# A decoder layer on one core: the feed-forward part as two stages of its own, its first product by Strassen's scheme

## The chip, the cores and the metric

The kernel runs on one core of one Trainium2 chip. The metric is the device time of one execution in microseconds. The time before is the median of three runs.

## What is computed

One inference step of a hybrid decoder layer, for a prompt of 2048 tokens and for 8 sample tokens, which share all weights. Everything is fp32. Cut to what matters here:

```python
h = rmsnorm(x)
u_ssm | u_pool | q_mem | gate_logits = h @ w_in
o_ssm  = S5 state-space model over time, GELU, GLU        # sequential over tokens
o_pool = trailing means of 2, 4, 8, 16 tokens, a linear map per group
o_mem  = cross-attention (4 heads) into 256 memory tokens; samples have their own cached keys and values
merged = sum_b sigmoid(gate_b) * (o_b @ w_branch_up[b])   # three branches
x = x + rmsnorm(merged @ w_out)
hf = rmsnorm(x) @ w_ffn_in                                # 1024 -> 2 x 2816
x = x + rmsnorm((silu(hf[:, :2816]) * hf[:, 2816:]) @ w_ffn_out)
```

## The kernel before, in words

Activations stand with the channel on the 128 partitions and tokens along the row. The prompt is worked in four blocks of 512 tokens (q = 0 to 3); the 8 sample tokens ride with block 1, which is therefore 520 wide and is computed in two column pieces of 256 and 264. fp32 accuracy comes from splitting each operand into a high and a low fp32r part (`split`, L167 to L169: ScalarE makes the high part, VectorE or, for the kinds in ON_POOL, GpSimd the low one), and three matmuls for each pair of tiles: high x high, high x low, low x high (`mmk`, L263). So a tile of 128 outputs over 1024 inputs is 8 x 3 matmuls for each column piece.

Weights come as tiles of at most 512 KB in one fixed order (`_weight_plan`), each loaded by SP and split three tiles ahead of its use (`wget`, `prefetch`, `w_emit`, L226 to L255), through four buffers each of wr, wh, wl. All DMAs are issued by SP.

Each block runs, in order: GLU of the S5 output; projections with memory attention and pooling (`projections`); gates and branch products for the three branches (`gates`, in block 0 in the order 2, 1, 0, later 0, 1, 2); the out-projection (`out_project`, L1187); the projection of u for the next block (`ssm_project`); then the residual with its norm (`residual`, L1204), which makes the split operand h2 of the feed-forward part. The feed-forward part follows for the same block in chunks of 5, 5, 6 and 6 column blocks: `ffn_in` (L1228) computes for each of 22 column blocks the gate half (fa) and the linear half (fb), 8 x 3 matmuls each, scales by the reciprocal norm, applies SiLU and splits the product; `ffn_out` (L1274) multiplies a chunk back, 8 output tiles, and adds the chunks in SBUF. `finish` (L1298) adds the last residual and stores.

Work that is not on the matmul stream is written as generators in a list called background; `step` issues the next piece of the first generator at marked places, `flush` all of what is left. The S5 recurrence of block q+1 (`s5_group`) is issued in steps within the feed-forward part of block q. `norm_stats` and `norm_apply` prepare the next block's input. In block 1 `sample_attention` (L1053) streams the samples' cached keys and values (56 transfers of 256 KB) in steps during the gates of branches 0 and 1; branch 2, which needs it, comes last. In the last block the out-projection and the last chunk of the second product run in two halves of 256 tokens, so that the tail is short.

The Tile framework orders each engine's instructions by a simulated time line with the order of writing as priority, and puts in the semaphores; PSUM has six banks under the tag pa and two under pb.

Of the kernel before, what the change touches and what calls it, by code (L numbers as in the profile page):

```python
# [19 lines left out]
P = 128  # L20
# [12 lines left out]
FCH = (5, 5, 6, 6)  # L33
FOFF = (0, 5, 10, 16)
# [9 lines left out]
STEPS = (1, 3, 1, 1)  # L44
# [4 lines left out]
NARROW = (QS, NQ - 1)  # L49
ORDER = ((2, 1, 0), (0, 1, 2), (0, 1, 2), (0, 1, 2))  # L50


def _weight_plan():
# [14 lines left out]
    ffn = []  # L68
    for c in range(len(FCH)):
        for f in range(FOFF[c], FOFF[c] + FCH[c]):  # L70
            ffn += [("fa", f), ("fb", f)]
        if c > 0:
            ffn += [("fo", c - 1, m) for m in range(KD)]
    ffn += [("fo", len(FCH) - 1, m) for m in range(KD)]
    seq = [("wk", h) for h in range(NH)] + [("wv", i) for i in range(4)] + us
    for q in range(NQ):
        if q > 0:
            seq += glu
        seq += proj
        for b in ORDER[q]:  # L80
            if q == 0 and b == 0:
                seq += glu
            seq += gates(b, q == 0 and b == 0)
        last = q + 1 == NQ
        seq += wo + wo if last else wo + us
        seq += ffn
        if last:
            seq += ffn[-KD:]
# [4 lines left out]
_STORED = [k for k in dict.fromkeys(_SEQ) if k[0] not in ("KT", "V")]  # L93
# [37 lines left out]
def trunk(ctx, tc, nc, I, O):  # L131
    V, S, G, T = nc.vector, nc.scalar, nc.gpsimd, Tensor(tc, nc)
    pool = ctx.enter_context(tc.tile_pool(name="sb", bufs=1))
# [3 lines left out]
    BUFS = {"h": 16, "br": 24, "acc": 8, "xr": 3, "U": 5, "G": 2, "tmp": 7, "rb": 1, "rb2": 1, "st2": 1,  # L137
            "ops": 6, "wr": 4, "wh": 4, "wl": 4}
    SIZE = {"tmp": 528, "ops": 512, "G": 512, "wr": 1024, "wh": 1024, "wl": 1024}
# [5 lines left out]
    def slot(tag, dt=F32):  # L145
        n = nm(tag)
        return pool.tile([P, SIZE.get(tag, W520)], dt, tag=tag, name=n, bufs=BUFS[tag])

    def small(shape, tag, bufs=1, dt=F32):
        n = nm(tag)  # L150
        return pool.tile(shape, dt, tag=tag, name=n, bufs=bufs)
# [31 lines left out]
    g_pre, g_post, g_fpre, g_fpost, g_mem = (gv[:, i, :] for i in range(5))  # L183
    cv = small([P, 2, NB], "cv")
# [14 lines left out]
    d_rb = dram([NQ, P, W520], "d_rb")  # L199

# [22 lines left out]
    seq = _SEQ  # L223
    wstate = {"emit": 0, "cur": 0, "buf": {}}

    def w_emit(i):  # L226
        key = seq[i]
        n = _ncols(key)
# [14 lines left out]
    def prefetch():  # L243
        i = wstate["cur"]
        while wstate["emit"] <= min(i + AHEAD, len(seq) - 1):
            w_emit(wstate["emit"])
            wstate["emit"] += 1
# [53 lines left out]
    def rsqrt_scaled(dst, sums, r, bl):  # L301
        v = slot("tmp")
        sl = slice(bl[0][0], bl[-1][0] + bl[-1][1])
        d, rr, vv = dst[:, sl], r[:, sl], v[:, sl]
        for o, n in bl:
            ps = psum2()
            T.matmul(ps[:, :n], lhsT=ones, rhs=sums[:, o:o + n], start=True, stop=True)
            V.tensor_tensor(v[:, o:o + n], r[:, o:o + n], ps[:, :n], MUL)
        V.tensor_tensor(vv, vv, rr, MUL)
        V.tensor_scalar(vv, vv, 1.0 / DM, EPS, MUL, ADD)  # L310
        rsqrt_core(d, vv, sl.stop - sl.start)
        V.tensor_tensor(d, d, rr, MUL)

    def rsqrt_rows(sums, bl, r=None):
        lo, hi = bl[0][0], bl[-1][0] + bl[-1][1]
        ns = -(-(hi - lo) // P)
# [4 lines left out]
        c = small([P, 3, 5], "rsq", 4)  # L321
        d, v, a = (c[:w, i, :ns] for i in range(3))
        if r is None:
            V.tensor_scalar(v, ps[:w, :ns], 1.0 / DM, EPS, MUL, ADD)
        else:
            V.tensor_tensor(v, ps[:w, :ns], r, MUL)
            V.tensor_tensor(v, v, r, MUL)
            V.tensor_scalar(v, v, 1.0 / DM, EPS, MUL, ADD)
# [6 lines left out]
        if r is not None:  # L335
            V.tensor_tensor(d, d, r, MUL)
# [715 lines left out]

    def sample_attention(qs, o_mem):  # L1053
# [7 lines left out]
        for b in range(NS):  # L1061
            qb = slot("U")
            nc.sync.dma_start(qb[:, :512].rearrange("p (h d) -> p h d", h=NH),
                              qv[b].unsqueeze(0).to_broadcast([P, NH, P]))
            for mt in range(2):
                kc = slot("U")
# [18 lines left out]
        for b in range(NS):  # L1085
            for hp in range(2):
                pb = slot("U")
                nc.sync.dma_start(pb[:, :512].rearrange("p (h m) -> p h m", h=2),
                                  dv[b, 2 * hp:2 * hp + 2].unsqueeze(0).to_broadcast([P, 2, NMEM]))
                vc = slot("U")  # L1090
# [4 lines left out]
        for m in range(NH):  # L1095
            hi, lo = o_mem[m]
            split(hi[:, TQ:W520], lo[:, TQ:W520], os_[:, :, m])
        yield

    def projections(q, h, br):  # L1100
# [3 lines left out]
        ns = 1 if q == 0 else 0  # L1104
# [39 lines left out]
    def gates(q, b, first, last, h, ob, acc, out, extra=None):  # L1144
        n = width(q)
        wub = None
        ahead = q == 0 and b == 0
# [39 lines left out]
    def out_project(q, mg, z, st, bl):  # L1187
        for m in range(KD):
            w = wget("wo", m)
            ps = [psum() for _ in bl]  # L1190
            mmk(q, ps, w, mg, bl=bl)
            if len(z) <= m:
                z.append(slot("acc"))
            sq = st if m == 0 else slot("tmp")
            for p_, (o, n) in zip(ps, bl):
                sl = slice(o, o + n)
                S.activation(sq[:, sl], p_[:, :n], AF.Square)  # L1197
                S.activation(z[m][:, sl], p_[:, :n], AF.Copy, scale=g_post[:, m:m + 1])
            sl = slice(bl[0][0], bl[-1][0] + bl[-1][1])
# [4 lines left out]
    def residual(q, z, st, st2, h2, bl):  # L1204
        rb = slot("rb")
        with T:
            (rsqrt_mean if q + 1 < NQ else rsqrt_quick)(rb, st, bl)
        yield
        sl = slice(bl[0][0], bl[-1][0] + bl[-1][1])
        for k in range(KD):  # L1210
# [318 lines left out]
```

## Time and profile before

| | |
|---|---|
| median of 3 runs | 3197.15 us (3193.63 to 3197.33) |
| span of the profiled execution | 3196.5 us; no separate time is listed for it, the median lies 0.65 us above |
| mean granted TensorE clock | 0.983 |
| moved by DMA | 393 MB, 123 GB/s mean |

The rows further down are read so: engines are PE (TensorE matmuls), PEld (its weight loads, which overlap), DVE (VectorE), ACT (ScalarE), POOL (GpSimd) and SP (which issues DMAs). L119 is the one line at which every matmul is recorded, so matmuls are told apart by tile names and shapes. Idle time of an engine that does not set the end costs nothing.

### The profile page before, as it was taken

Reading aid. Unit: us, or ns where it says so; the run is one execution under the profiler, and the core shown is the slowest. Engines: PE = TensorE matmul, PEld = TensorE weight load, DVE = VectorE, ACT = ScalarE, POOL = GpSimd, SP = SyncE. Lnnn points to the kernel's source line nnn. Section 1 sums busy time; section 2 is a strip of 40 time slices with the busy share of each in tenths; the row PEclk is TensorE's granted clock in tenths of the full one; section 3 lists DMA queues with packets and bytes.
Section 4 is the critical chain, followed back from the end, with each engine's and each line's share of the span. In section 5 each row is a group of like instructions: output and inputs, shape, how many; then the busy total and the mean of one; then the engine's idle time right before and its main releaser. Section 6 shows DMA issues by size and latency. Waiting matters only on the chain.

```text
span 3196.5 us, 43801 instructions
## 1 busy us (share of the span) xinstructions
PE 3071.6 (96%) x17043; PEld 2651.8 (83%) x17043; DVE 1879.6 (59%) x2905; ACT 1122.9 (35%) x1791; POOL 855.7 (27%) x690
## 2 busy tenths in 40 slices
PE   8889999999989899899999999999999999999997
PEld 6778877888888799899998888788888788888887
DVE  7877768555485635755548544764556833563346
ACT  4532433322344224323224423433223522533222
POOL 2565242111154403211114311421112501620112
PEclk9999999999999999999999999999999999999999
DMA  6354444323347633433324432533323333432233
GB/s 204 110 167 136 143 127 141 112 88 106 100 144 178 212 98 119 142 95 113 109 76 142 153 112 92 165 114 114 106 86 125 125 99 95 146 124 92 90 115 105
DMA packets 174735, 393.14 MB, mean 123 GB/s; under 512 B 39680, under 2 KB 51520, under 8 KB 174528
## 3 DMA queue, kind: packets, MB, share of 16 engines
q1 hardware_dynamic: 174528, 390.35, 38.7%
q8 instruction: 134, 2.20, 0.3%
q14 instruction: 73, 0.60, 0.1%
HBM read 362.41 MB, written 27.55 MB: 122 GB/s over the span
## 4 chain that ended last, share of the span: by engine, by line
PE 83%; DVE 9%; DMA 3%; issue 1%; ACT 1%; POOL 1%; SPq 1%; DVEq 0%; POOLq 0%; ACTq 0%
PE pa L119 79%; PE pb L119 3%; DVE acc L1319 1%; PE pb L122 1%; DVE acc L1213 1%; DVE wl L169 1%; DVE tmp L419 1%; DMA U<-in_cv_t 1%; SPq L660 1%; DMA U<-in_ck 0%; DMA d_ops<-br 0%; DVE tmp L289 0%; DVE rb L290 0%; DMA ops<-d_ops 0%; DVE tmp L288 0%
## 5 line engine op out<-in xcount | busy, mean ns | idle before, releaser
L119 PE MATMUL pa<-h,wh 128*128 128x512 f32 (+2 forms) x6144 | 1568.3, 352 | 30.0 <-DVE h L1221 17.1
L119 PEld LDWEIGHTS pa<-h,wh 128*128 128x128 f32 x6144 | 1040.3, 191 | 189.9 <-DVE h L1221 19.6
L168 ACT ACTIVATE wh<-wr 128x1024 fp32r<-128x1024 f32 (+3 forms) x572 | 568.2, 994 | 1557.7 <-PE pa L119 1186.3
L119 PE MATMUL pa<-h,wl 128*128 128x512 f32 (+2 forms) x3072 | 983.5, 351 | 0.7 <-POOL wl L169 0.7
L119 PE MATMUL pa<-br,wh 128*128 128x512 f32 (+2 forms) x3848 | 929.8, 340 | 20.7 <-ACT wh L168 8.3
L169 DVE TENSOR_TENSOR wl<-wr,wh 128x1024 fp32r<-128x1024 f32 (+3 forms) x476 | 572.7, 1203 | 370.9 <-ACT wh L168 360.0
L119 PEld LDWEIGHTS pa<-br,wh 128*128 128x128 f32 x3848 | 635.5, 189 | 106.1 <-ACT wh L168 8.5
L119 PEld LDWEIGHTS pa<-h,wl 128*128 128x128 f32 x3072 | 546.5, 190 | 79.5 <-POOL wl L169 1.0
L119 PE MATMUL pa<-br,wl 128*128 128x512 f32 (+2 forms) x1924 | 596.2, 340 | 1.0 <-DVE wl L169 1.0
L1265 POOL TENSOR_TENSOR tmp<-tmp,tmp 128x512 f32<-128x512 f32 (+1 forms) x88 | 150.5, 1712 | 934.5 <-ACT tmp L1264 934.5
L169 POOL TENSOR_TENSOR wl<-wr,wh 128x1024 fp32r<-128x1024 f32 (+1 forms) x96 | 238.7, 2493 | 514.3 <-ACT wh L168 482.9
L119 PEld LDWEIGHTS pa<-br,wl 128*128 128x128 f32 x1924 | 340.7, 189 | 42.9 <-DVE wl L169 1.4
L1267 DVE TENSOR_TENSOR tmp<-tmp,pa 128x512 f32<-128x512 f32 (+1 forms) x110 | 61.8, 579 | 230.4 <-PE pa L119 225.8
L1263 DVE TENSOR_TENSOR tmp<-rb,pa 128x512 f32<-128x512 f32 (+1 forms) x110 | 61.5, 578 | 193.1 <-PE pa L119 188.2
L1288 DVE TENSOR_TENSOR acc<-acc,pa 128x512 f32<-128x512 f32 (+2 forms) x128 | 68.7, 552 | 152.5 <-PE pa L119 152.3
L1181 POOL TENSOR_TENSOR acc<-acc,tmp 128x512 f32<-128x512 f32 (+1 forms) x32 | 48.5, 1519 | 224.6 <-DVE tmp L1179 206.0
L168 ACT ACTIVATE br<-tmp 128x512 fp32r<-128x512 f32 (+1 forms) x120 | 75.7, 633 | 75.3 <-DVE tmp L1267 31.6
L169 DVE TENSOR_TENSOR br<-tmp,br 128x512 fp32r<-128x512 f32 (+1 forms) x120 | 90.6, 756 | 4.7 <-ACT br L168 4.5
L1201 DVE TENSOR_TENSOR tmp<-tmp,tmp 128x512 f32<-128x512 f32 (+2 forms) x35 | 62.9, 1796 | 48.7 <-ACT tmp L1197 48.6
L119 PE MATMUL pa<-wh,h 128*128 128x512 f32 x256 | 84.6, 406 | 4.4 <-DVE h L376 2.3
L1179 DVE TENSOR_TENSOR tmp<-tmp,pa 128x512 f32<-128x512 f32 (+1 forms) x80 | 44.8, 579 | 65.0 <-PE pa L119 63.6
L1214 POOL TENSOR_TENSOR acc<-acc,xr 128x512 f32<-128x512 f32 (+2 forms) x40 | 57.3, 1448 | 80.5 <-DVE acc L1213 61.0
(316 smaller groups left out, 2626.9 us busy)
## 6 DMA issues: line engine op xcount, KB each, us to landing
wr<-in_w_all SPq DMA_DIRECT2D x424, 512.0 KB, 3.4
ops<-d_ops SPq DMA_DIRECT2D x112, 256.0 KB, 3.6
wr<-in_w_all SPq DMA_DIRECT2D x72, 384.0 KB, 3.0
xr<-in_x_t SPq DMA_DIRECT2D x96, 256.0 KB, 3.5
wr<-in_w_all SPq DMA_DIRECT2D x64, 320.0 KB, 2.8
d_ops<-br SPq DMA_DIRECT2D x28, 256.0 KB, 2.7
out_y_t<-acc SPq DMA_DIRECT2D x24, 256.0 KB, 3.6
d_x<-acc SPq DMA_DIRECT2D x16, 256.0 KB, 3.3
```

The costliest lines, as they stand in the source:

```text
L119: self._done(self.nc.tensor.matmul(*a, **k))
L122: self._done(self.nc.tensor.transpose(*a, **k))
L168: S.activation(dst_hi, src, AF.Copy)
L169: (eng or V).tensor_tensor(dst_lo, src, f(dst_hi), SUB)
L1179: V.tensor_tensor(t[:, sl], t[:, sl], u_, MUL)
L1181: (V if last else G).tensor_tensor(acc[j][:, :n], acc[j][:, :n], t[:, :n], ADD)
L1201: V.tensor_tensor(st[:, sl], st[:, sl], sq[:, sl], ADD)
L1214: G.tensor_tensor(zk, zk, xt[:, sl], ADD)
L1263: V.tensor_tensor(t[:, sl], rb2[:, sl], a_, MUL)
L1265: G.tensor_tensor(t[:, :n], t[:, :n], sg[:, :n], MUL)
L1267: V.tensor_tensor(t[:, sl], t[:, sl], b_, MUL)
L1288: V.tensor_tensor(zz, zz, p_[:, :n], ADD)
```

## The change

The kernel becomes three stages. Stage one is the mixing part of all four blocks, one after another, each followed at once by the projection of u for the next. All blocks now take the branches in the order 2, 1, 0, with GLU ahead of branch 0; S5 and the residual of the block before are background work of the projections and gates, in more steps (STEPS, NS1). The samples' attention has to be complete ahead of the gates of branch 2, the first ones of block 1, and uses the eight acc buffers instead of the five U buffers. The residual now also writes the reciprocal norm to DRAM.

Stage two computes the first feed-forward product for two pairs of blocks, (0, 1) and (2, 3), 1024 tokens each; the samples are divided over blocks 0 and 1 (516 columns), blocks 2 and 3 have 512. `sums` (a background generator, for the first pair in stage one) scales the stored residuals, makes Strassen-Winograd's sums of token half and channel half, and stores seven operands of four tiles each in d_S. `left` loads and splits these 28 tiles through xr. For each of the 22 column blocks `w_pair` loads fa and fb and makes the sums of weights. Seven products of 4 k x 3 passes x 2 column halves are accumulated in three pairs of PSUM banks, of which X is read three times in between. The gated products go to DRAM (d_f).

Stage three runs the second product block by block over all 22 input tiles at once (`load_f`, 44 split tiles held), in two column halves side by side, for the last block one half after the other. SBUF of the stages is shared by pools that follow each other; a tile waits only for the tiles whose place it takes.

```diff
-FCH = (5, 5, 6, 6)
+FCH = (8, 8, 6)
+SB = ((0, 1), (2, 3))
-STEPS = (1, 3, 1, 1)
+STEPS = (1, 2, 2, 2)
+NS1 = (1, 7, 1, 1)
-ORDER = ((2, 1, 0), (0, 1, 2), (0, 1, 2), (0, 1, 2))
+ORDER = (2, 1, 0)
...
+    BUFS = {"U": 5, "G": 2, "ops": 6, "h": 16, "br": 24, "acc": 8, "rb2": 1,
+            "xr": 4, "tmp": 7, "rb": 1, "wr": 4, "wh": 4, "wl": 4, "wt": 2,
+            "ev": 4, "S": 56, "f": 52, "z": 8}
...
+    def w_pair(f):
+        wa, wb = w_load(("fa", f)), w_load(("fb", f))
+        t21, t34 = slot("wt"), slot("wt")
+        L, R = slice(0, BW), slice(BW, 2 * BW)
+        V.tensor_tensor(t21[:, R], wb[:, L], wa[:, L], SUB)
+        V.tensor_tensor(t21[:, L], wb[:, R], t21[:, R], SUB)
+        V.tensor_tensor(t34[:, L], wb[:, R], wb[:, L], SUB)
+        V.tensor_tensor(t34[:, R], wa[:, R], t21[:, L], SUB)
+        for src in (wa, t21, t34, wb[:, R]):
+            hi, lo = slot("wh", F32R), slot("wl", F32R)
+            split(hi[:, :n], lo[:, :n], src)
...
             if i == 3 and q == QS:
-                background.append(sample_attention(qs, o_mem))
-                step(2)
+                background.insert(len(background) - 1, sample_attention(qs, o_mem))
...
+    def sums(sb):                       # 4 k: four scaled tiles, four sums, seven stores
+            V.tensor_tensor(s1, A[1, 0], A[1, 1], ADD)
+            V.tensor_tensor(s3, A[0, 0], A[1, 0], SUB)
+            V.tensor_tensor(s2, s1, A[0, 0], SUB)
+            V.tensor_tensor(s4, A[0, 1], s2, SUB)
+            for i, t in enumerate((A[0, 0], A[0, 1], s4, A[1, 1], s1, s2, s3)):
+                nc.sync.dma_start(d_S[sb, i, k, :, :n], t)
...
+    PRODUCTS = (0, 1, 5, 4, 6, 3, 2)
+    def left(sb):
+        for i in PRODUCTS:
+            for k in range(KH):
+                raw = slot("xr")
+                nc.sync.dma_start(raw[:, :n], d_S[sb, i, k, :, :n])
+                hi, lo = slot("S", F32R), slot("S", F32R)
+                split(hi[:, :n], lo[:, :n], raw[:, :n])
...
+    def ffn_in(sb, got):                # for each of 22 column blocks f_
+            B11, B21, T2, T1, T3, t4, B22 = wget("f1", f_)
+            product(X, 0, B11, True)
+            take(p1)                    # ScalarE reads both banks of X
+            product(Z, 1, B21, True)
+            plus(p1, Z)                 # VectorE adds both banks of Z
+            step()
+            product(X, 5, T2, False)
+            take(u2)
+            product(Y, 4, T1, True)
+            step()
+            product(X, 6, T3, False)
+            take(u3)
+            plus(u3, Y)
+            product(X, 3, t4, False)
+            both(f1_)                   # sigmoid of X, times X
+            product(Y, 2, B22, False)
+            plus(u2, Y)
+            S.activation(f0[:, :n], p1[:, :n], AF.Sigmoid)
+            G.tensor_tensor(f0[:, :n], f0[:, :n], p1[:, :n], MUL)
+            for i, (ft, b) in enumerate(((f0, u2), (f1, u3))):
+                V.tensor_tensor(ft[:, :n], ft[:, :n], b[:, :n], MUL)
+                nc.sync.dma_start(d_f[SB[sb][i], f_, :, :n], ft[:, :n])
+            step()
...
     for q in range(NQ):
-        if q > 0:
-            br[0] = glu(q, yT)
-            step(1)
...
+            if b == 0:
                 flush()
                 br[0] = glu(q, yT)
             if b == 2 and q == QS:
-                flush()
+                while "samples" not in done:
+                    step()
...
+            if i == 0 and q + 1 == NQ:
+                background.append(sums(0))
...
+        out_project(q, mg, z, st)
+        flush()
+        res = residual(q, z, st)
         if q + 1 < NQ:
+            background.append(res)
             U, us = ssm_project(q + 1, h)
             background.append(s5(q + 1, U, us, yT))
+        else:
+            run(res)
...
+    for sb in range(len(SB)):
+        prefetch()
+        got = left(sb)
+        if sb + 1 < len(SB):
+            background.append(sums(sb + 1))
+        ffn_in(sb, got)
+        flush()
...
+    for q in range(NQ):
+        ft = load_f(q, n)
+        for bl in ([[(0, n // 2), (n // 2, n // 2)]] if q + 1 < NQ else [[x] for x in HALVES]):
+            ffn_out(ft, bl, z, st)
+            flush()
+            background.append(finish(q, z, st, bl))
```

## Rows read from the trace of the kernel before

**Rows 1.** The page, busy time of each engine with share of the span.

```profile
PE 3071.6 (96%) x17043; PEld 2651.8 (83%) x17043; DVE 1879.6 (59%) x2905; ACT 1122.9 (35%) x1791; POOL 855.7 (27%) x690
```

**Rows 2.** The chain of waits: start us, us, what; block 0, block 1, the last half.

```profile
801.35 89.13 PE pa L119 x384
...
1330.19 46.09 PE pa L119 x384
...
3142.91 21.03 PE pa L119 x177
```

**Rows 3.** The page's costliest groups: busy us, mean ns | idle before; weight loads.

```profile
L119 PEld LDWEIGHTS pa<-h,wh 128*128 128x128 f32 x6144 | 1040.3, 191 | 189.9 <-DVE h L1221 19.6
```

**Rows 4.** Stretches at hand-overs: length, busy PE, PEld, DVE, ACT, POOL, clock, DMA, GB/s.

```profile
889.00:952.00 63.00, 53.69 (x396) 51.97 (x395) 56.90 (x79) 29.84 (x67) 30.27 (x19) 0.92 0.48 151
...
1268.00:1315.00 47.00, 40.60 (x240) 36.21 (x238) 39.73 (x49) 18.78 (x38) 14.32 (x9) 0.93 0.50 154
...
1705.00:1760.00 55.00, 48.32 (x217) 39.86 (x217) 52.30 (x64) 24.19 (x47) 26.68 (x15) 0.91 0.45 143
...
2040.00:2090.00 50.00, 43.32 (x180) 34.09 (x179) 41.86 (x47) 19.74 (x41) 16.23 (x9) 0.93 0.46 154
...
2458.00:2513.00 55.00, 47.83 (x206) 38.90 (x205) 52.64 (x61) 23.46 (x44) 29.11 (x16) 0.91 0.46 147
...
2799.00:2842.00 43.00, 37.99 (x252) 35.02 (x253) 29.23 (x71) 14.28 (x28) 6.41 (x8) 0.92 0.46 147
```

**Rows 5.** The same view: block 0's S5, block 1's samples, block 2's gates, its feed-forward.

```profile
112.00:250.00 138.00, 118.93 (x559) 96.83 (x558) 106.90 (x291) 51.19 (x89) 87.40 (x185) 0.94 0.47 147
...
952.00:1004.00 52.00, 45.51 (x345) 44.12 (x345) 34.53 (x61) 28.59 (x60) 30.00 (x28) 0.97 0.67 155
1004.00:1115.00 111.00, 95.68 (x753) 94.19 (x752) 61.24 (x87) 26.01 (x46) 49.28 (x35) 0.94 0.69 207
...
1800.00:1996.00 196.00, 196.00 (x845) 158.27 (x844) 81.75 (x87) 59.48 (x75) 26.61 (x17) 1.00 0.33 105
...
2090.00:2458.00 368.00, 368.00 (x1685) 301.37 (x1684) 202.94 (x280) 114.80 (x154) 62.31 (x37) 1.00 0.34 108
```

**Rows 6.** Groups by line and shape, VectorE: busy us, mean ns | idle before.

```profile
L169 DVE TENSOR_TENSOR wl<-wr,wh 128x1024 fp32r<-128x1024 f32 x344 | 454.3, 1321 | 334.0 <-ACT wh L168 323.7 <-PE pa L119 5.7
L169 DVE TENSOR_TENSOR br<-tmp,br 128x512 fp32r<-128x512 f32 x90 | 68.4, 762 | 2.5 <-ACT br L168 2.5
...
L795 DVE TENSOR_TENSOR_SCAN G<-r,carry_re,G 128x128 f32<-128x128 f32 x64 | 44.2, 746 | 7.9 <-POOL G L788 7.8
...
L289 DVE TENSOR_TENSOR tmp<-tmp,tmp 128x512 f32<-128x512 f32 x24 | 21.8, 907 | 0.5
...
L1213 DVE TENSOR_TENSOR acc<-acc,rb 128x512 f32<-128x512 f32 x16 | 20.8, 1368 | 0.1
...
L1288 DVE TENSOR_TENSOR acc<-acc,pa 128x256 f32<-128x256 f32 x40 | 16.7, 417 | 41.4 <-PE pa L119 41.2
...
L784 DVE TENSOR_TENSOR G<-ops,pb 128x512 f32<-128x512 f32 x16 | 11.0, 686 | 7.1 <-PE pb L119 3.9 <-DMA ops<-d_ops 2.9
```

**Rows 7.** The same view, ScalarE.

```profile
L168 ACT ACTIVATE wh<-wr 128x1024 fp32r<-128x1024 f32 x432 | 457.4, 1060 | 1164.9 <-PE pa L119 846.8 <-issue 275.3 <-POOL acc L1320 14.2
...
L168 ACT ACTIVATE br<-tmp 128x512 fp32r<-128x512 f32 x90 | 56.6, 631 | 53.4 <-DVE tmp L1267 24.0 <-DVE tmp L960 21.0 <-DVE tmp L917 7.5
...
L1178 ACT ACTIVATE tmp<-pa 128x256 f32<-128x256 f32 x16 | 5.8, 365 | 0.0
```

**Rows 8.** The same view, GpSimd.

```profile
L1214 POOL TENSOR_TENSOR acc<-acc,xr 128x512 f32<-128x512 f32 x16 | 27.3, 1717 | 43.3 <-DVE acc L1213 30.5 <-DMA xr<-in_x_t 9.4 <-DVE h L1221 3.3
...
L1068 POOL TENSOR_TENSOR U<-U,U 128x512 f32<-128x512 f32 x16 | 21.3, 1344 | 29.7 <-DMA U<-in_ck 29.4
```

**Rows 9.** DMA issues: KB each, median us from issue to landing.

```profile
xr<-in_x_t SPq DMA_DIRECT2D x96, 256.0 KB, 3.5
...
U<-in_ck SPq DMA_DIRECT2D x16, 256.0 KB, 6.2
```

More of the change, by code (lines that the diff above doesn't have):

```diff
@@ L183, in trunk @@
     g_pre, g_post, g_fpre, g_fpost, g_mem = (gv[:, i, :] for i in range(5))
+    mix = tc.tile_pool(name="mix", bufs=1, reuse_waits="tile")
+    stage[0] = mix.__enter__()
     cv = small([P, 2, NB], "cv")
@@ L199, in trunk @@
     d_rb = dram([NQ, P, W520], "d_rb")
+    d_rb2 = dram([NQ, P, W520], "d_rb2")
+    d_S = dram([len(SB), 7, KH, P, HW_], "d_S")
+    d_f = dram([NQ, NF, P, HW_], "d_f")
     background = []
@@ L244, in prefetch @@
         i = wstate["cur"]
-        while wstate["emit"] <= min(i + AHEAD, len(seq) - 1):
+        while wstate["emit"] < len(seq):
+            pair = seq[wstate["emit"]][0] == "f1"
+            if wstate["emit"] > i + (1 if pair else AHEAD) or pair and stage[0] is not half[0]:
+                break
             w_emit(wstate["emit"])
@@ L299, in rsqrt_mean, with rsqrt_rows @@
         rsqrt_core(dst[:, sl], v[:, sl], sl.stop - sl.start)
[L301 to L314, printed above, removed]
+    def rsqrt_rows(sums, bl):
         lo, hi = bl[0][0], bl[-1][0] + bl[-1][1]
-        ns = -(-(hi - lo) // P)
+        ns = next(i for i in range(-(-(hi - lo) // P), 99) if (hi - lo) % i == 0)
         w = (hi - lo) // ns
@@ L1097, in sample_attention @@
             split(hi[:, TQ:W520], lo[:, TQ:W520], os_[:, :, m])
+        done.add("samples")
         yield
@@ L1146, in gates @@
         wub = None
-        ahead = q == 0 and b == 0
+        ahead = b == 0
         opened = []
@@ new lines, in residual @@
+    def residual(q, z, st):
+        n = width(q)
+        rb = slot("rb")
+        rsqrt_mean(rb, st, blocks(q))
+        st2 = slot("rb2")
+        yield
+        for k in range(KD):
+            xt = load_x(q, k)
+            zk = z[k][:, :n]
+            V.tensor_tensor(zk, zk, rb[:, :n], MUL)
+            G.tensor_tensor(zk, zk, xt[:, :n], ADD)
+            nc.sync.dma_start(d_x2[q, k, :, :n], zk)
+            sq = st2 if k == 0 else slot("tmp")
+            S.activation(sq[:, :n], zk, AF.Square)
+            if k > 0:
+                V.tensor_tensor(st2[:, :n], st2[:, :n], sq[:, :n], ADD)
+            yield
+        rb = slot("rb")
+        rsqrt_mean(rb, st2, blocks(q))
+        nc.sync.dma_start(d_rb2[q, :, :n], rb[:, :n])
+        yield
@@ L1298, in finish @@
-    def finish(q, z, st, scale, bl, x2):
-        last = q == NQ - 1
-        sl = slice(bl[0][0], bl[-1][0] + bl[-1][1])
-        if last:
-            r2, w, _ = scale
-            c0 = sl.start // w
-            rows = rsqrt_rows(st, bl, r2[:, c0:c0 + (sl.stop - sl.start) // w])
-            rb = spread(rows, 0)[:, :sl.stop - sl.start]
+    def finish(q, z, st, bl):
+        sl = slice(bl[0][0], bl[-1][0] + bl[-1][1])
+        if q + 1 == NQ:
+            rb = spread(rsqrt_rows(st, bl), 0)[:, :sl.stop - sl.start]
@@ L1306, in finish @@
         else:
             rb = slot("rb")
-            rsqrt_scaled(rb, st, scale, bl)
+            rsqrt_quick(rb, st, bl)
             rb = rb[:, sl]
@@ L1429, in trunk @@
     nc.sync.dma_start(O["pp"], hist)
+    mix.__exit__(None, None, None)
+    second = tc.tile_pool(name="half", bufs=1, reuse_waits="tile")
+    stage[0] = half[0] = second.__enter__()
+    slot("ev")
+    for sb in range(len(SB)):
+        prefetch()
[4 more added lines that the diff above has]
+        flush()
+    second.__exit__(None, None, None)
+    down = tc.tile_pool(name="down", bufs=1, reuse_waits="tile")
+    stage[0] = down.__enter__()
+    slot("z")
+    for q in range(NQ):
+        n = fwidth(q)
+        ft = load_f(q, n)
+        z = []
+        st = slot("tmp")
+        for bl in ([[(0, n // 2), (n // 2, n // 2)]] if q + 1 < NQ else [[x] for x in HALVES]):
+            ffn_out(ft, bl, z, st)
+            flush()
+            background.append(finish(q, z, st, bl))
+    flush()
+    down.__exit__(None, None, None)
 _OUTS = {
```

338 lines of the change are left out of this document (155 added, 183 removed).

## The prediction

> **What bounds the kernel now.** I read the page's busy times first: TensorE is busy 96% of the span, VectorE 59%, the other two about a third or less [rows 1]. The engine's share alone says nothing of its rate, so next I read the chain of waits, for stretches in which it holds nothing but matmuls. A 512-column matmul costs 89.13/384 = 0.2321 us, a pair of blocks of 256 and 264 columns 46.09/384 = 0.1200 us each, and a stretch of 256 columns alone 21.03/177 = 0.1188 us [rows 2]. For 258 columns I interpolate 0.1194 (an estimate). Every matmul has its own weight load beside it; a load is listed at 0.191 us and still the 256-column matmuls follow each other at 0.119 [rows 2, 3], so loads are hidden.
>
> The table of stretches then shows where TensorE is not full. In the long feed-forward stretch and in the gates it is full to the last digit, while VectorE works 203 of 368 us and 82 of 196 [rows 5]. It is not full where one part hands over to the next: feed-forward to the next block's mixing, mixing to feed-forward [rows 4], and in the second block's projections and gates, where the samples' attention runs [rows 5]. So two things can move the time: the number of matmul columns, and what waits at each hand-over.
>
> **Part 1, matmul columns.** First product before: 22 column blocks x 2 halves (fa, fb) x 8 x 3 = 1056 matmuls of 512 columns in blocks 0, 2, 3, and 2112 narrow ones in block 1: 3 x 1056 x 0.2321 + 2112 x 0.1200 = 988.8 us. After: 7 products x 4 k x 3 passes x 2 halves = 168 matmuls of about 256 columns for 1024 tokens; 22 x 168 = 3696 for each pair of blocks: 3696 x 0.1194 + 3696 x 0.1188 = 880.4. That is **-108.4**: one eighth less work, of which about 2% of the rest is given back, since two matmuls of 256 cost 0.238 where one of 512 costs 0.232.
> Second product before: 528 x 0.2321 (blocks 0, 2) = 122.5 each, 126.7 (block 1), 123.3 (block 3, last chunk in halves): 495.1. After, everything in halves: 4 x 1056 at 0.1188 to 0.1194 = 503.1. **+8.0.** The last out-projection in one piece saves 1.0. Sum **-101.4** [rows 2].
>
> What weighs against this is the doubled count of weight loads. The rows show the answer: 384 narrow matmuls, each with its load, at 0.120 us [rows 2, 3]. The Trainium skill, "TensorE: Matmul & The Clock Gate", section on packing small matmuls ("The mechanism"), says that a weight load overlaps matmuls in flight only when it is for other row groups; all loads here fill all rows, so by that rule none would be hidden. The trace disagrees; what the rule would cost stands among the rivals.
>
> **Part 2, the other engines in the new stages.** For one column block (168 matmuls, 20.0 us) VectorE has four sums of weights at 0.76, splits 3 x 1.32 + 0.76, eight half-width reads of PSUM at 0.42 and two products at 0.76: 12.6 us [rows 6]. ScalarE has some 8, GpSimd one. The accumulators X are read by ScalarE while the next product goes elsewhere, except between the sixth product (T3) and t4: there a half is read in 0.365 [rows 7] and has the other half's 12 x 0.119 = 1.43 us. A weight split in the way adds up to 1.06 [rows 7]. I take 0.1 us a block, 5 in all; nothing to 30 are the ends. Transfers: weights of the first product are fetched twice instead of four times (-46 MB), d_S and d_f are written and read (+76 MB), all through SP; the feed-forward stretch now uses a third of the DMA engines [rows 5], so that is hidden in steady state, not at the stage starts.
>
> **Part 3, hand-overs removed.** The six stretches at hand-overs leave TensorE idle for 9.3 + 6.4 + 6.7 + 6.7 + 7.2 + 5.0 = 41 us (length less busy) [rows 4]. Matmul ends are modelled, so short waits hide in the busy time: by count, the first holds 396 x 0.120 = 47.5 of 63 us, so 15.5 is lost, and the fourth 180 x 0.2321 = 41.8 of 50, so 8.2. I scale to **-63**; the floor is 41. Finish, rescaling and the h split leave these places.
>
> **Part 4, hand-overs and waits added.**
> - *Mixing to mixing, three times.* Out-projection and the projection of u follow as before, but the S5 part loses its feed-forward cover and must end before glu, together with the residual. VectorE in that window: S5 4 x (12 x 0.69 + 8 scans at 0.75) = 57; residual 8 x (1.37 + 0.76) + 2 x 9 x 0.91 of rsqrt = 33; 28 weight splits x 1.32 = 37; some 52 operations of scores, projections, pooling and gates at 0.69 = 36: 163 us [rows 6] beside (252 + 576) x 0.2321 = 192 us of matmuls. It fits at 85%, crowded in the projections. S5's 28 operator loads and the residual's 16 transfers move along on SP, their sums on GpSimd; there DMA is at a third and GpSimd at 27 of 196 us [rows 5]. Ends: nothing, and 36 us each (rival B). Nearest rows are the present hand-overs to mixing, 7 to 15 us with finish in the residual's place [rows 4]; without glu at the front I take 8 each: **+24**.
> - *Samples' attention.* It now must end before the first gates of block 1, not the last. 56 transfers of 256 KB at the 207 GB/s of that stretch are 71 us [rows 5]; GpSimd's 32 products at 1.34 are 43 [rows 8]. Eight buffers instead of five shorten what the landing of 6.2 us [rows 9] adds. Four remaining projections, attention and a gate give some 45 us of matmuls, so 26 us stall, and every weight load stands behind those transfers on SP. Today the two stretches lose 6.5 + 15.3 = 22 [rows 5]. **+4**, ends -15 and +30.
> - *Mixing to the Strassen stage.* Sums of blocks 0 and 1 are made in the background, but their 28 tiles come through the four xr buffers, which the last residual's x tiles hold. After the last out-projection: rsqrt 9 x 0.91 = 8, five tiles at GpSimd's 1.72 until a buffer is free, landing 3.5, split 1.4; then 28 tiles at some 1.3 us ((3.5 + 1.4) / 4 buffers, slightly delayed by the residual on VectorE): 22 + 36 + the last product's 3, less the 20 that this column block takes anyway [rows 6, 7, 8, 9]. **+42**; ends 12 (tiles loaded ahead) and 60.
> - *Between the two pairs:* the same 28 tiles, but buffers come free during the last column block; VectorE has 28 x 0.76 more in some 40 us that already hold 25. **+8** (0 to 15). *To the second product and between its blocks:* 22 tiles at 1.3 against 15.8 us in which they are used, started one output tile early: **+3 and 3 x 2** (0 to 20 together).
> - *In-stage stalls* +5 (above). *Tail:* four xr buffers instead of preloaded tiles, one landing: **+3** (0 to 6).
>
> Sum of added: 24 + 4 + 42 + 8 + 9 + 5 + 3 = 95. **Total:** 3196.5 - 101.4 - 63 + 95 = 3127. The profiled span is 0.65 us under the median of 3197.15, too little to correct for.
>
> **Rivals.**
> *A, nearly every hand-over is covered* (0.17). For: TensorE is full wherever its inputs were ready early [rows 5], transfers need not wait for the residual if buffers are handed out otherwise. Then mixing costs nothing at its joins, the stage start 12, pair and block joins 3: 3196.5 - 101.4 - 63 + 12 + 3 + 5 + 3 = 3055. Against: the four xr buffers.
> *B, VectorE becomes the bound of the mixing* (0.15), the slower side. Place: projections and two thirds of the gates of blocks 1 to 3. For: the only stretch today that runs S5 without feed-forward cover, 112 to 250, leaves TensorE idle 19 of 138 us with VectorE at 77% [rows 5]. At that share, 14% of 259 us of projections and gates is 36 us a block, 3 x (36 - 8) = 84 more: **3211**. It makes the change slower from 31 us a block on. Against: that stretch also builds the S5 operators through several DMA round trips, which later blocks don't.
> *C, weight loads are not hidden at half width* (0.01): 11616 narrow matmuls replace 8064 of both widths; at 0.191 us for each of the 3552 loads more, less 192 in the out-projection, 640 us: about 3770. [rows 2, 3] speak against it.
>
> **How the numbers follow.** Forecast 0.67, its own range 3080 to 3185 from the ends of the stage start, the joins and the samples; A 0.17, B 0.15, C 0.01. To hold 8 in 10 the range goes halfway into A and to where B begins: 3055 to 3200. About 0.2% (6 us) is what a measurement of this kernel can tell. Faster by more: 0.65 + 0.17 + 0.02 = 0.84; within: 0.03; slower: 0.13.
>
> **What would show it.** Right: stretches of nothing but matmuls in the new stage at 0.119 us, 20.0 us a column block; no idle TensorE at three mixing joins beyond some 8 us; one hole of some 40 us behind the last out-projection, its waits on splits of S behind xr transfers; ScalarE's reads of X not on the chain. Wrong: a pitch above 0.122 in the new stage, ends of products waiting for PSUM reads; TensorE waiting for weight splits through the gates of blocks 1 to 3 (B); no hole at the stage start (A); samples' attention stalling over 50 us.

## The result, and the profile after

The changed kernel takes **3232.3 us** (median of four runs, 3229.2 to 3236.1), beside 3196.6 for the kernel before on the same chip: a ratio of 1.0117, 95% interval 1.0103 to 1.0132. It is slower by 36 us where 70 us faster was forecast, and lies outside the range. The profiled execution has a span of 3228.5 us.

The page's busy times, as in [rows 1]; then, from the chain of waits (start us, us, what), its long stretches of nothing but matmuls, as in [rows 2]:

```profile
PE 3006.1 (93%) x20319; PEld 2766.3 (86%) x20319; DVE 1904.3 (59%) x3143; ACT 1208.1 (37%) x2091; POOL 732.9 (23%) x630
```

```profile
2263.08 419.71 PE pa L116 x3544
...
2711.26 125.32 PE pa L116 x1038
```

TensorE is busy for 65 us less, and the span is 32 us longer: it stands still for about 97 us more (222 against 125, span less busy). By the columns of the forecast 101 us of busy time would have gone; some 36 of them went into slower matmuls, at a mean granted clock of 0.960 where it was 0.983. The gain is there: 419.71/3544 is 0.1184 us a matmul, each with a load of its own. What was lost must stand elsewhere. The table of stretches (length, then busy us and count of PE, PEld, DVE, ACT, POOL; granted clock, DMA share, GB/s) finds it, as [rows 4, 5] did before:

```profile
500.00:560.00 60.00, 36.84 (x260) 33.51 (x259) 52.11 (x101) 20.82 (x44) 23.62 (x18) 0.75 0.42 137
560.00:593.00 33.00, 28.06 (x160) 25.89 (x161) 20.24 (x50) 13.93 (x36) 10.35 (x11) 0.67 0.22 53
593.00:636.00 43.00, 19.25 (x98) 16.03 (x96) 24.74 (x43) 8.34 (x15) 31.53 (x29) 0.72 0.77 216
636.00:678.00 42.00, 17.52 (x126) 16.52 (x127) 25.30 (x54) 8.95 (x21) 21.10 (x18) 0.66 0.69 233
1000.00:1012.00 12.00, 6.95 (x34) 5.11 (x32) 11.06 (x12) 4.57 (x13) 8.88 (x6) 0.98 0.48 157
1160.00:1190.00 30.00, 14.86 (x71) 13.09 (x70) 16.06 (x31) 5.63 (x10) 6.28 (x5) 0.66 0.12 42
1553.00:1583.00 30.00, 14.93 (x69) 13.01 (x68) 17.96 (x34) 4.66 (x8) 5.02 (x4) 0.66 0.32 101
1740.00:1800.00 60.00, 26.71 (x114) 20.90 (x113) 46.23 (x61) 19.44 (x31) 13.33 (x8) 0.66 0.42 134
...
2200.00:2260.00 60.00, 60.00 (x502) 60.00 (x502) 43.42 (x72) 32.19 (x59) 3.91 (x3) 1.00 0.50 159
2260.00:2680.00 420.00, 419.84 (x3547) 419.56 (x3546) 230.37 (x385) 157.80 (x283) 27.33 (x22) 1.00 0.29 87
2680.00:2702.00 22.00, 16.93 (x114) 15.41 (x113) 12.57 (x20) 10.37 (x17) 1.17 (x1) 0.92 0.64 198
```

Read it from below. The Strassen stage is full, the joint of its two pairs (2200 to 2260) too, and the second product's start loses 5 us. The hole behind the last out-projection (1740 to 1800) is there, as forecast. Most of the rest is in the mixing of blocks 1 to 3, which now follow each other without a feed-forward part between: 76 us of standing still in block 1 between 500 and 678, and 15 us each at the end of the S5 part of blocks 2 and 3. VectorE is crowded in the first of these, 52 of 60 us, and in the short wait from 1000 to 1012, 11 of 12; there this table can't tell an engine with too much to do from one with the wrong thing first. In the others it is busy for 53 to 61% of the time, and the transfers reach 0.7 to 0.8 only where the samples' tiles stream (593 to 678): no engine is full, they wait for each other. Two places in the timeline (start us, us, engine, line, out<-in, how many; in brackets the idle time before and what ended it) show how. First, block 1's query projection:

```profile
503.31 11.30 DVE L1230 TENSOR_TENSOR acc<-acc,rb 128x512 f32<-128x512 f32 x8
504.08 13.87 POOL L1231 TENSOR_TENSOR acc<-acc,xr 128x512 f32<-128x512 f32 x8 [4.81 <-DVE acc L1230]
...
516.74 0.74 DVE L1008 TENSOR_TENSOR br<-pa,br 128x256 fp32r<-128x256 f32 x2
...
517.21 0.80 PE L116 MATMUL pa<-h,wh 128*128 128x256 f32 x2 [12.70 <-DVE br L1008]
```

Seven background pieces are issued at one place (NS1), and the residual of block 0 is first in the list. So its eight rescalings stand in a row in VectorE's order, and with one weight split behind them (2.28 us from 514.54) ahead of L1008, which splits the projected queries out of PSUM. TensorE waits 12.70 us for that split. Second, the end of block 2's S5 part:

```profile
1158.97 0.61 PE L116 MATMUL pb<-ops,G 128*128 128x128 f32 x4
...
1166.80 3.78 PE L116 MATMUL pb<-U,ops 128*128 128x128 f32 x16 [1.32 <-ACT U L784]
1168.91 0.69 DVE L799 TENSOR_TENSOR G<-ops,pb 128x512 f32<-128x512 f32 x1 [4.72 <-PE pb L116]
...
1172.75 2.59 DVE L810 TENSOR_TENSOR_SCAN G<-r,carry_re,G 128x128 f32<-128x128 f32 x4 [0.85 <-POOL G L803]
...
1179.51 0.68 DVE L824 TENSOR_TENSOR G<-tmp,tmp 128x508 f32<-128x508 f32 x1
...
1180.29 1.44 PE L116 MATMUL pb<-ops,G 128*128 128x128 f32 x4 [9.23 <-issue]
...
1181.94 1.06 PE L116 MATMUL pb<-ops,G 128*128 128x128 f32 x4
...
1186.74 0.73 PE L116 MATMUL pa<-h,wh 128*128 128x512 f32 x2 [1.17 <-ACT tmp L1195]
```

From 1159 to 1186.7 TensorE's order holds nothing but the end of one S5 group and the whole of the last; no gate matmul stands between, though gates follow. So the group's chain (transpose, copy, matmul, products, scans, products, matmul) is waited for link by link. The list puts "issue" as the releaser of the 9.23 us; L824, which ends at 1180.19, is what it waited for. In the kernel before the same chains ran under the feed-forward columns.

And the waits of TensorE between 500 and 680 us (for what: us in total, times, longest), the largest:

```profile
PE pa L116 <- ACT br L170: 14.8, 1, 14.8
PE pa L116 <- DVE br L1008: 12.7, 1, 12.7
PE pb L119 <- DVE ys L860: 8.5, 1, 8.5
PE pb L119 <- DVE sc L1086: 8.3, 1, 8.3
```

The first and the last are the samples' attention (its result, its scores), the third a piece of the S5 part that stands on VectorE among the reductions of the samples' products.

### The profile page after: what moved, and what is told of

It reads as the page before. It is cut to its first block, busy times and chain, and to the rows that moved or that the text cites. A ratio compares the mean times of both kernels' runs of the same rounds, so it can differ in the third digit from the quotient of the medians.

```text
span 3228.5 us, 51314 instructions
## 1 busy us (share of the span) xinstructions
PE 3006.1 (93%) x20319; PEld 2766.3 (86%) x20319; DVE 1904.3 (59%) x3143; ACT 1208.1 (37%) x2091; POOL 732.9 (23%) x630
## 5 line engine op out<-in xcount | busy, mean ns | idle before, releaser
L116 PE MATMUL pa<-S,wh 128*128 128x258 f32 (+1 forms) x4928 | 892.4, 284 | 8.7 <-DVE S L171 4.6
L170 ACT ACTIVATE wh<-wr 128x1024 fp32r<-128x1024 f32 (+1 forms) x460 | 458.5, 997 | 1036.0 <-PE pa L116 801.9
L116 PEld LDWEIGHTS pa<-S,wh 128*128 128x128 f32 x4928 | 760.6, 189 | 14.7 <-DVE S L171 7.4
L116 PE MATMUL pa<-h,wh 128*128 128x512 f32 (+2 forms) x2560 | 672.8, 358 | 31.4 <-DVE br L1008 12.7
L116 PE MATMUL pa<-S,wl 128*128 128x258 f32 (+1 forms) x2464 | 692.6, 282 | 0.0
L116 PEld LDWEIGHTS pa<-h,wh 128*128 128x128 f32 x2560 | 440.2, 193 | 101.5 <-DVE br L1008 12.9
L116 PE MATMUL pa<-br,wh 128*128 128x512 f32 (+2 forms) x1864 | 480.3, 353 | 35.9 <-ACT br L170 15.7
L116 PE MATMUL pa<-f,wh 128*128 128x258 f32 (+1 forms) x2816 | 468.2, 283 | 5.9 <-DVE f L171 3.0
L116 PEld LDWEIGHTS pa<-S,wl 128*128 128x128 f32 x2464 | 468.2, 190 | 0.3 <-DVE wl L171 0.2
L116 PE MATMUL pa<-h,wl 128*128 128x512 f32 (+2 forms) x1280 | 420.4, 356 | 0.8 <-DVE wl L171 0.8
```

Source lines behind the costliest of these rows:

```text
L116: self._done(self.nc.tensor.matmul(*a, **k))
L170: S.activation(dst_hi, src, AF.Copy)
```

## The experiments

Three theories. **Theory 1, order and cover:** background pieces are put into the engines' orders faster than their chains can run, with nothing beside them. **Theory 2, arrival:** the tiles of a stage come too late. **Theory 3, load:** VectorE has too much to do (rival B). Each expectation numbers its own theories, and its theory 2 is often load; outside of them the numbers are the ones given here. Unless said, each edit is made in the changed kernel.

**Slow pace in block 1's projections.**

```diff
-NS1 = (1, 7, 1, 1)
+NS1 = (1, 1, 1, 1)
```

> Edit: in block 1 one background piece behind each projection instead of seven. The changed kernel took 3232 us; between 480 and 690 us of its span TensorE loses some 107 us. Theory 1 (order): seven pieces at once put whole S5 chains of one group into TensorE's order between two projections, and it waits through scans and GELU; of the 47 us lost before the samples' attention begins (500 to 590) some 15 stay, the samples' 60 stay: 3195 to 3210. Theory 2 (load): VectorE has too much to do in block 1 whatever the order; the same work must end before GLU, so 3225 to 3240. Rival: the samples' attention, now issued in one piece ahead of the gates, costs more than is won: above 3240.

Measured 3211.1 us, ratio 1.0045 [1.003, 1.006]: 21 us off. TensorE's largest waits between 500 and 660 us:

```profile
PE pb L119 <- DVE sc L1086: 35.2, 1, 35.2
PE pa L116 <- ACT br L170: 30.3, 1, 30.3
PE pa L116 <- DVE br L1008: 3.2, 1, 3.2
```

That is a microsecond above the range that the expectation gave to order, and 14 below that of load. The wait for L1008 falls from 12.7 to 3.2 us, as theory 1 has it. What is left is bare: 65 us for the samples' attention alone, first its scores, then its result.

**The samples' attention left out** (its rows are zeros), in the changed kernel and, later, in the kernel before.

```diff
 def sample_attention(qs, o_mem):
+    while None in o_mem:
+        yield
+    os_ = small([P, NS, NH], "os")
+    G.memset(os_, 0.0)
+    ...
```

> Edit: the samples' attention is left out (its output columns are zeros); background pieces stand where they did in the changed kernel (3232 us). Theory 1 (its chain of transfers stands ahead of the first gates of block 1): the loss between 590 and 690 goes, -50 to -65 us: 3167 to 3182. Theory 2 (S5's chains hold TensorE there anyway): 3215 to 3232.

Measured 3176.1 us, ratio 0.9932 [0.9917, 0.9947]: 56 us off.

> The kernel before with the samples' attention left out (its output rows are zeros), as the earlier experiment did in the changed kernel, where it took 56 us off. Theory 1 (lost cover): before, this work lay under the feed-forward products of block 1 and cost next to nothing, so the time stays at 3190 to 3199 us. Theory 2 (the work costs its time wherever it stands, by the transfers or by GpSimd and VectorE): 3135 to 3165 us.

Measured 3178.3 us, ratio 0.9943 [0.9926, 0.9961]: 18 us off, between the two theories. In the kernel before TensorE waits once for the samples' scores, and its stretch from 1030 to 1060 us fills without them. First TensorE's wait there in the kernel before, then the stretch before and in this run:

```profile
PE pb L122 <- DVE sc L1069: 11.7, 1, 11.7
```

```profile
1030.00:1060.00 30.00, 17.86 (x133) 17.35 (x132) 15.87 (x23) 5.49 (x9) 12.39 (x10) 0.83 0.68 181
```

```profile
1030.00:1060.00 30.00, 30.00 (x251) 30.00 (x250) 9.35 (x14) 8.29 (x14) 0.00 (x0) 1.00 0.25 77
```

So the same work costs 18 us in the one kernel and 56 in the other; the change made it 38 us dearer. The lost cover is the reason that the two bare waits of the run before point to; its buffers and the pieces beside it changed as well, and these were not told apart.

**The S5 pieces of block 1 by themselves:** the samples left out as above, and one piece a step.

```diff
-STEPS = (1, 2, 2, 2)
-NS1 = (1, 7, 1, 1)
+STEPS = (1, 1, 2, 2)
+NS1 = (1, 1, 1, 1)
```

> The changed kernel with the samples' attention left out (zeros in its rows) and one background piece a step in block 1 throughout (seven a projection and two a gate step before). It asks what the S5 pieces of block 1 cost by themselves, beside the samples. Without the samples the kernel took 3176 us, and TensorE then still stood some 57 us between 500 and 640 us. Theory 1 (pieces put into TensorE's order faster than VectorE makes their operands): most of that goes, 3125 to 3145 us. Theory 2 (the pieces cost VectorE's or the transfers' time at any pace): over 3160 us.

Measured 3133.9 us, ratio 0.9804 [0.9787, 0.982]: 42 us off the 3176.1. The two stretches, first with the fast pace, then with the slow one:

```profile
500.00:560.00 60.00, 37.15 (x247) 33.55 (x247) 50.55 (x96) 20.83 (x44) 23.63 (x18) 0.76 0.42 133
560.00:640.00 80.00, 71.00 (x494) 66.98 (x493) 51.37 (x118) 35.53 (x79) 29.14 (x31) 0.82 0.33 83
```

```profile
500.00:560.00 60.00, 53.10 (x392) 50.65 (x391) 50.46 (x97) 36.01 (x88) 38.89 (x35) 0.94 0.54 156
560.00:640.00 80.00, 80.00 (x698) 78.14 (x697) 59.08 (x133) 25.84 (x47) 8.89 (x9) 1.00 0.46 139
```

VectorE works 50 of 60 us in both first rows, and TensorE 37 or 53. The pages of the two runs, again first the fast pace, give the load of the whole execution:

```profile
PE 3000.2 (95%) x20316; PEld 2762.7 (87%) x20316; DVE 1876.2 (59%) x3107; ACT 1208.0 (38%) x2088; POOL 695.6 (22%) x599
```

```profile
PE 2979.1 (95%) x20316; PEld 2745.1 (88%) x20316; DVE 1875.4 (60%) x3107; ACT 1204.1 (38%) x2086; POOL 696.2 (22%) x599
```

VectorE's load is the same, 1876.2 and 1875.4 us, the order isn't: theory 1, against theory 3. The 42 us are those of both edits together, NS1 and STEPS.

**The pace in the gates of blocks 2 and 3,** faster and slower.

```diff
-STEPS = (1, 2, 2, 2)
+STEPS = (1, 2, 3, 3)
```

> Edit: in blocks 2 and 3 three background pieces per half gate instead of two, so that S5's 44 pieces with the residual end within five or six of branch 2's eight gates, and branch 1's gates run without them. The changed kernel (3232 us) loses some 21 us in each of these blocks where branch 2 ends. Theory 1 (order: S5's four groups are chains of some 30 us each, in TensorE's order, squeezed into too few matmuls): worse, 120 us of chain beside some 50 of gates: 3250 to 3310. Theory 2 (VectorE's load): the same work before the same GLU, 3225 to 3240. Theory 3 (the tmp buffers that S5 holds keep branch 1's gates from being read): better, 3195 to 3215.

Measured 3238.2 us, ratio 1.0128 [1.0111, 1.0145]: 6 us more, far less than the expectation's theory 1 (order) had for it, and inside the range that it gave to load. The slower pace tells the two apart.

```diff
-STEPS = (1, 2, 2, 2)
+STEPS = (1, 2, 1, 1)
```

> Edit: in blocks 2 and 3 one background piece per half gate instead of two, so that S5 is spread over the gates of both branches (some 134 us of matmuls beside chains of 120). Theory 1 (order): most of the 21 us in each block goes: 3190 to 3205. Theory 2 (VectorE's load): 3225 to 3240. Theory 3 (tmp buffers): S5 now stands beside all of branch 1, the loss stays or grows: 3232 to 3260.

Measured 3206.1 us, ratio 1.0027 [1.0017, 1.0038]: 26 us off. Its stretches at the end of S5 in block 2, and at GLU in block 3:

```profile
1130.00:1190.00 60.00, 60.00 (x298) 50.01 (x297) 38.75 (x56) 18.14 (x25) 14.76 (x11) 1.00 0.40 127
1590.00:1626.00 36.00, 19.38 (x77) 15.26 (x76) 20.66 (x29) 7.98 (x11) 0.00 (x0) 0.77 1.01 295
```

This is a microsecond above the range of order, and 19 below that of load. Block 2 has no hole any more, with VectorE no less busy than before (39 of these 60 us; 34 in the changed kernel, where TensorE stands 15 of them). In block 3 a new one of 17 us comes up where GLU's `flush` issues, behind S5, also the sums for the Strassen stage, which had been put into the list behind the first gates: DMA at 1.01, 295 GB/s. So the last S5 group in a row, as the timeline shows it, and not arrival or load, makes the hole at the end of S5. Why pace 2 makes the scheduler write it in a row and pace 1 doesn't stays open; the dose is not even, since pace 3 adds little to pace 2.

**The hole before the Strassen stage,** two tries: the second norm of the last residual moved into the stage (the sum of its squares, L1236, is what ended the hole), and then also the last residual's x tiles in other buffers and the stage's first loads and splits at a higher priority. In the changed kernel the first load of S, the first splits and the matmul of that norm stand so:

```profile
1769.47 0.43 SPq L1288 DMA_DIRECT2D xr<-d_S  x1
1774.66 1.14 ACT L170 ACTIVATE S<-xr 128x516 fp32r<-128x516 f32 x2
1778.77 2.04 PE L116 MATMUL pb<-rb,ones 128*128 128x512 f32 x2 [26.88 <-DVE rb L1236]
```

The first edit:

```diff
+        if q + 1 == NQ:
+            nc.sync.dma_start(d_rb2[q, :, :n], st2[:, :n])
+            return
         rb = slot("rb")
         rsqrt_mean(rb, st2, blocks(q))
...
```

> Edit: the reciprocal norm of block 3's residual is made in the second stage (from sums stored in DRAM, nine pieces late), so that its ones-matmul no longer stands between the last out-projection and the first product. The changed kernel has a hole of 27 us there that ends with that matmul. Theory 1 (TensorE's order: the matmul waits for the residual's whole chain): the hole falls to some 5 us, 3205 to 3212. Theory 2 (as forecast: the tiles of S come late through the xr buffers, which the residual holds): the hole moves to the first products and at most 5 us are won, 3227 to 3232.

Measured 3233.8 us, ratio 1.0114 [1.0099, 1.0129]: nothing. Then, added to it:

```diff
...
-            xt = load_x(q, k)
+            xt = load_x(q, k, tag="h" if q + 1 == NQ else "xr")
...
+                with tc.high_priority(offset=0 if sb else 400):
...
```

> Edit: besides moving the last ones-matmul (which alone left the hole of 27 us in place), the last residual's x tiles go to free h buffers instead of xr, and loads and splits of the first 28 S tiles are put ahead of the residual in the order of each engine. Theory 1 (the S tiles wait for xr and behind the residual, as the forecast had it): the hole falls to 5 to 8 us, the first column block is then fed at 1.3 us a tile; of 46 us lost around the start some 20 to 28 are won: 3204 to 3212. Theory 2 (the places of S in SBUF come free only late): nothing is won, 3228 to 3234.

Measured 3233.4 us, ratio 1.0109 [1.0094, 1.0124]: nothing either. TensorE's wait in the first run, then the timeline of the second:

```profile
PE pa L116 <- ACT S L170: 30.7, 2, 26.7
```

```profile
1780.56 0.63 ACT L1234 ACTIVATE tmp<-acc 128x512 f32<-128x512 f32 x1 [1.04 <-POOL acc L1231]
1781.10 1.20 ACT L170 ACTIVATE S<-xr 128x516 fp32r<-128x516 f32 x2
1781.77 0.50 PEld L116 LDWEIGHTS pa<-S,wh 128*128 128x128 f32 x2 [24.25 <-ACT S L170]
1783.07 0.63 ACT L170 ACTIVATE S<-xr 128x516 fp32r<-128x516 f32 x1 [0.77 <-DMA d_x<-acc]
```

The first two splits of S have no wait of their own: they begin when ScalarE has finished the last square of the residual (L1234), behind which they are queued, and their loads had been issued by 1628. So with the norm and the loads out of the way, the splits still stand in ScalarE's order behind the whole residual, though the edit asked for them to go first. The third waits 0.77 us for a store of the residual's result (d_x<-acc), whose place in SBUF it takes. That is what the expectation's theory 2 (the places of S come free late) says, and its range holds the measured time. Whether late places or the order alone keep the first two splits back isn't shown; a version with places of their own for them wasn't tried.

**Block 1 in another order:** branch 1 before branch 2, so that the samples' attention has the gates of branch 1 as cover, its pieces woven two to one with those of S5, its tiles in free br buffers, and another pace (NS1, STEPS).

```diff
-STEPS = (1, 2, 2, 2)
-NS1 = (1, 7, 1, 1)
+STEPS = (1, 3, 2, 2)
+NS1 = (1, 1, 1, 1)
...
-ORDER = (2, 1, 0)
+ORDER = ((2, 1, 0), (1, 2, 0), (2, 1, 0), (2, 1, 0))
...
-                kc = slot("acc")
+                kc = slot("br")
...
-                background.insert(len(background) - 1, sample_attention(qs, o_mem))
+                background[-1] = weave(sample_attention(qs, o_mem), background[-1])
```

> Edit: block 1 takes its branches in the order 1, 2, 0, the samples' attention runs through free br buffers, two of its pieces to one of S5, behind the projections and branch 1's gates (one piece behind each projection, three steps at each half gate). Theory 1 (order and place, not load): the 107 us lost in block 1 fall to 30 to 45, total 3155 to 3175. Theory 2 (VectorE's load in block 1 is the bound): at most 20 us are won, 3210 to 3232. Rival: the chains of S5 and of the samples are longer than two branches' gates (some 200 against 200 us): 3180 to 3210.

Measured 3175.7 us, ratio 0.9932 [0.9914, 0.9951]: 57 us off, and faster than the kernel before, with the whole computation in it. The edits were made together; of the 57 us, NS1 alone had given 21.

**All of it together,** written as an edit of the kernel just shown: that order and weave, pace 1 in blocks 2 and 3, and the sums for the Strassen stage put into the list only behind GLU, where the last branch's gates cover them.

```diff
-STEPS = (1, 3, 2, 2)
+STEPS = (1, 3, 1, 1)
...
                 br[0] = glu(q, yT)
+                if q + 1 == NQ:
+                    background.append(sums(0))
...
-            if i == 0 and q + 1 == NQ:
-                background.append(sums(0))
```

> The changed kernel with the order of block 1's branches, the weave of the samples' attention and the pace of one S5 piece a step in blocks 2 and 3 together, and the last block's sums for the Strassen stage queued behind its gated branch. Theory 1 (what is lost in the mixing is the order and pace of the background pieces): the gains add, 3235 - 57 - 26 and up to 17 more for the sums: 3130 to 3155 us. Theory 2 (the pieces only move the loss to the next place without cover): over 3165 us.

Measured **3127.6 us**, ratio 0.9785 [0.9769, 0.98]: 105 us off the changed kernel and 69 off the kernel before. The gains add, and a little more: 2 us below the expected range. Its mixing stretches of blocks 2 and 3, and block 1 below:

```profile
1010.00:1125.00 115.00, 115.00 (x580) 96.42 (x580) 75.98 (x116) 31.87 (x43) 21.17 (x16) 1.00 0.42 135
1390.00:1500.00 110.00, 110.00 (x551) 92.13 (x550) 74.41 (x115) 32.12 (x44) 22.32 (x16) 1.00 0.40 136
```

```profile
500.00:560.00 60.00, 49.37 (x356) 46.09 (x355) 53.62 (x96) 36.24 (x88) 38.09 (x35) 0.92 0.58 165
560.00:630.00 70.00, 64.29 (x504) 62.41 (x504) 53.75 (x98) 18.33 (x32) 28.96 (x20) 0.92 0.62 190
630.00:700.00 70.00, 63.27 (x530) 60.88 (x529) 55.34 (x118) 18.35 (x34) 35.37 (x27) 0.95 0.69 229
```

Blocks 2 and 3 are full, with S5, residual and all; block 1 still stands 23 of these 200 us.

**One block product twice,** to price the term that the change is made for (the first layer's result is another one by that).

```diff
             product(Y, 2, B22, False)
+            product(Y, 2, B22, False)
```

> The changed kernel with the last of each column block's seven products done twice (the first layer's result is another one by that). It prices a block product: 44 x 24 more multiplications. Theory 1 (the Strassen stage is bound by TensorE's columns alone, at 0.1184 us a multiplication): +125 us, 3350 to 3365 us. Theory 2 (evictions or the pieces' loads hold part of the stage, so that an eighth product is partly free): under 3335 us.

Measured 3357.8 us, ratio 1.0505 [1.0488, 1.0522]: 125.5 us more for 1056 matmuls, 0.119 us each. The chain in the stage's second half gives 482.61/4076 = 0.1184:

```profile
2329.70 482.61 PE pa L116 x4076
```

The stage is bound by TensorE's columns, as theory 1 of this run says; no part of an eighth product is free.

## Why the prediction was wrong, step by step

- **Part 1 (matmul columns, -101.4) held.** The pitch in the new stage is 0.1184 where 0.1188 to 0.1194 was taken, and a block product costs 125.5 us by itself. Rival C is out: a load for every narrow matmul, all rows filled, and still 0.1184. By the rule of the Trainium skill, "TensorE: Matmul & The Clock Gate", section "The mechanism", as the prediction put it, 3552 more loads would have shown; this trace doesn't agree with it. The same section of the Trainium skill also names a background weight buffer, which the prediction passed over; no run here shows whether that is what hides the loads.
- **Part 2 (in-stage, +5) and the joint of the pairs (+8) were a little too dear:** 420 of 420 and 60 of 60 us busy.
- **Part 3 (-63) can't be read off by itself.** The hand-overs went with the parts that they joined, and with them 41 us of idle time; the other 22 were an estimate that no run prices.
- **Part 4, the start of the Strassen stage (+42), came out near its size, with a mechanism that is only part of it.** TensorE stands 33 us between 1740 and 1800, at a granted clock of 0.66. The prediction had the tiles late behind the x tiles in the xr buffers, and in the changed kernel they are: the first load of S goes out at 1769.47, the first split starts at 1774.66. But two runs that took away the norm and then the x tiles changed nothing: the splits stand behind the residual in ScalarE's order, for a reason that stays open.
- **Part 4, "mixing to mixing" (+24), failed.** It weighed VectorE's work against the matmuls of the window, 163 in 192 us, found that it fits, and took 8 us a join from hand-overs of today. The work does fit: VectorE is busy for 1876 us with the loss in block 1 and for 1875 without. What the sum left out is that pieces stand in each engine's order at fixed places. Block 1 issues seven at once, a choice that stands in the diff (NS1) and got no line in the prediction. A slower pace took 42 us off in block 1 (with the samples left out) and 26 in blocks 2 and 3: at least 68 in place of 24.
- **Part 4, the samples' attention (+4), failed by size.** The sum of 71 us of transfers over 45 of cover gave 26 us of stall against 22 today, so that the move looked free. It costs 56 us where it stands now and 18 before: +38. Both stalls were mis-sized. The cover was counted as if attention and gates could run beside the stream; with the other pieces paced out, TensorE waits 35.2 and 30.3 us for it, the better part of those 71 us.
- **What the runs account for:** 44 us more than forecast at the joins and 34 at the samples are 78 of the 105 us that the forecast missed. How the 98 us of block 1 fall to pace and samples depends on which is taken away first: NS1 alone gave 21 with the samples in place, and leaving these out after it, with STEPS slower too, 77. The other 27 were not told apart; some of them are shorter waits in the mixing (5 of 12 us at 1000 to 1012, for one), and Part 3's estimate may be others.
- **Rival B had the place and the sign, and not the mechanism.** Its 3211 us came from VectorE's share in block 0. The pace runs speak against load: the same work in an even order takes 42 us less. The sign that it named, TensorE waiting for weight splits, is not among the waits between 500 and 680. Its chance of 0.15 was too small because the one row that showed S5 without feed-forward cover [rows 5] was explained away by the operators built there.
- **Slips in the working** change the forecast little: the terms of +42 add up to 41, and the two stretches that were counted scale 41 us to 61 and not 63. Rival B's 259 us are the projections and all three gates, where its place names two thirds of the gates; with those 192 us it would stand at 3184.
- The version with everything in order takes 3127.6 us, the number of the forecast, but not for its reasons: its terms differ, and the match is chance.

## What to carry to other kernels

When a change takes the long matmul stretches away from between short stages, list what ran under them, chain by chain: the question is not whether an engine's work fits into the window, but what stands in front of what in each engine's order, and how long one chain is from link to link. A background list must be issued at the pace of its chains, and what is due first needs its own cover; the pace of block 1's pieces was worth 21 us with the samples beside them and one edit, 42 without the samples and with both. If a large gain doesn't show, price it by itself (a product done twice) before looking for the loss: then the whole difference has to be somewhere else.

## What the runs showed of the hardware

**A short wait costs more than itself.** In the second timeline above four matmuls of 128 columns take 0.61 us at 1158.97 and 1.06 at 1181.94, after waits of 3.4, 1.3 and 9.2 us; the granted clock of that stretch is 0.66 on the mean, between its levels of 1.2 and 2.4 GHz. From 560 to 593 us TensorE is busy 28 of 33 us, at a clock of 0.67: there much of the loss is in matmuls at the lower level and not in idle time at all. The two pages of the pace run without the samples price it: with the same 20316 matmuls, 21 of the 43 us between the spans are TensorE's busy time (3000.2 and 2979.1 us), at mean clocks of 0.968 and 0.977. The Trainium skill, "TensorE: Matmul & The Clock Gate", section on HAM oscillation, describes waits, there for transfers, after which the next matmuls begin throttled; here the waits are links of a chain, and the slower matmuls behind them (0.61 against 1.06 us) agree.

**VectorE's rescaling of the residual takes more than twice as long beside GpSimd.** L1230 takes 0.67 us at the least and 1.75 in the median. In the residual of block 0 the first two of the eight take 0.69 us each, and the other six, beside GpSimd's additions (L1231, from 504.08 on), 1.75; L815, with operands of the same shape, takes 0.68 in the median. The list of line L1230 (ns min, median and max, first and last start):

```profile
L1230 DVE TENSOR_TENSOR acc<-acc,rb x32: 671/1746/1814, 503.3 to 1769.6; 128x512 f32<-128x512 f32 x24, 128x520 f32<-128x520 f32 x8
```

That is what made the eight rescalings ahead of L1008 11.3 us long where eight at 0.69 would be 5.5. The Trainium skill, "SBUF — State Buffer", section on who interferes with whom, has an instruction of VectorE with both inputs in SBUF and a reading one of GpSimd hold one port in turns; the two modes fit that.
